# A two-layer decoder trunk: the split input at four offsets, and five small tiles allocated elsewhere

## Chip, cores and metric

The kernel runs on one core of a Trainium2 chip. The metric is the device time of one execution in microseconds (us). Of the kernel before, three runs are shown: 1055.95, 1058.14 and 1058.58 us, median 1058.14 us. One further execution was profiled; it took 1055.96 us.

## What is computed

Two layers (DEPTH = 2) over a sequence of 256 tokens of width 1024, all in float32. Each layer is a token mixer and a SwiGLU block, both with a residual and a LayerNorm:

```python
for l in range(DEPTH):
    h = _mixer(x, w_in[l], w_gla_a2[l], b_gla_a[l], gla_norm_g[l], ret_norm_g[l],
               w_branch[l], b_gate[l], w_out[l])
    x = _layer_norm(ALPHA * x + h, ln1_g[l], ln1_b[l])
    f = _swiglu(x, w_gate[l], w_up[l], w_down[l])
    x = _layer_norm(ALPHA * x + f, ln2_g[l], ln2_b[l])
```

The mixer multiplies x by one wide matrix `w_in` and feeds three branches from it (gated linear attention, retention, dilated window attention) and three gates of width 1024; the gated sum of the branches goes through `w_out`. So x is read as a matmul operand in four places, which this text calls stages: stage 0 is the mixer of layer 0, stage 1 the SwiGLU of layer 0, stage 2 the mixer of layer 1, stage 3 the SwiGLU of layer 1.

## The kernel before

**Split operands.** Every float32 matmul operand is held as two parts in the type F32R: a high part and what is left of it. A product takes three matmuls: high by high, high by low and low by high. The input x lies transposed (128 partitions, 8 blocks k of 256 tokens) in the two tiles XH and XL (lines 284 and 285), 8192 bytes of each partition. They are allocated once, and all four stages use them: at the start `start_split` fills them, and at the end of each sub-layer `ln_rest` (lines 439 to 470) writes the next stage's x over the old one. Matmuls reach them through `xh(k)` and `xl(k)` (lines 377 to 381).

**Weights.** They come in 340 units of 128 x 1024 by DMA through six staging tiles, and ScalarE and VectorE split each into a pair of blocks out of a ring of 24 (`r0` to `r23`, 4096 bytes of each partition each). The blocks lie directly behind each other, so all begin at the same place modulo 512 bytes.

**Two forms of matmul on x.** `a_pair` (line 408) holds a 128 x 128 piece of the weights in TensorE and moves x past it, 256 columns at a time; it serves the queries and keys of the dilated branch, the gates and most of the SwiGLU. `b_unit` (line 388) holds 128 tokens of x and moves the weights past it, 512 columns at a time:

```python
mm(o, hi[:, c0:c0 + 128], rh(k), start=(i == 0 and j == 0), stop=False)   # a_pair
mm(o, hi[:, c0:c0 + 128], rl(k), start=False, stop=False)
mm(o, lo[:, c0:c0 + 128], rh(k), start=False, stop=(i == n - 1 and j == 3))
...
mm(ps, a, wh, start=(k == 0), stop=False)                                 # b_unit
mm(ps, a, wl, start=False, stop=False)
mm(ps, b, wh, start=False, stop=(k == 2 * n - 1))
```

The second argument of `mm` is held, the third moves past it. Products without x have the same two forms: `a_pair` on the branch outputs (line 1014) and `down` (line 1094) move and hold blocks of the ring only. Every matmul is recorded on line 130 of the profile, every transpose on line 134, and work of VectorE and ScalarE on line 118, since helpers issue them.

**Order of work.** The program is written by hand in one order per engine; a small model of the engines' clocks (`issue`, `settle`, `tick`) decides while the program is built where the side work of the branches is put between the big products.

**The small tiles.** `half` and `one` hold constants (lines 365 and 367); `m0`, `m1`, `den0` and `den1` hold softmax maxima and sums, 48 bytes each (lines 894 and 895); `junk` (line 751 in the mixer's `gla_all`) takes the squares that nobody reads, when ScalarE sums them for a norm.

Of the kernel before, what the change touches and what calls it, by code (L numbers as in the profile page):

```python
# [9 lines left out]
F32R = mybir.dt.float32r  # L10
# [6 lines left out]
S = 256  # L17
L = 2
H = 4
FF = 2816  # L20
KT = D // 128
# [33 lines left out]
def trunk(ctx: ExitStack, tc: tile.TileContext, wst, xt_in, x_in, cst, tri, pcol, wga, wa2, lnp, out):  # L55
# [5 lines left out]
    def T(shape, tag, bufs=1, dt=F32):  # L61
        return sb.tile(shape, dt, tag=tag, name=tag, bufs=bufs)
# [65 lines left out]
    def mm(out, lhsT, rhs, **k):  # L128
        issue("P", [out], [lhsT, rhs], size(out) * (4 if lhsT.dtype == F32 else 1) / 2.4 + 3)
        return nc.tensor.matmul(out, lhsT, rhs, **k)  # L130

    def transpose(out, in_):
        issue("P", [out], [in_], size(out) * 2 / 2.4 + 3)
        return nc.tensor.transpose(out, in_, ident)  # L134
# [5 lines left out]
    def settle(*aps, margin=MARGIN):  # L140

        while any(when(written, a, "P") + margin > clk["P"] for a in aps):
            yield
# [95 lines left out]
    def free(u):  # L239
        assert u == state["freed"]  # L240
        R.put(*parts.pop(u))
        state["freed"] += 1
# [4 lines left out]
    def spawn(g):  # L247
        side.append(g)
# [32 lines left out]
            yield  # L281


    XH = T([128, KT, S], "xh", 1, F32R)
    XL = T([128, KT, S], "xl", 1, F32R)
    xts = [F2.main()[0] for _ in range(4)]


# [2 lines left out]
    def start_piece(i):  # L291
        a, b = PIECES[i]
        return a, b, xts[a // 2].rearrange("p (k t) -> p k t", k=2)[:, a % 2:a % 2 + b - a, :]
# [4 lines left out]

    def start_split(i):
        a, b, xs = start_piece(i)  # L300
        act(XH[:, a:b, :], xs, AF.Copy)
        stt(XL[:, a:b, :], xs, 1.0, XH[:, a:b, :].bitcast(F32), op0=OP.mult, op1=OP.subtract)

# [56 lines left out]
    def cs(name):  # L360
        a, b = COLS[name]
        return C[:, a:b]

    ident = cs("ident")
    half = T([128, 4], "half")
    V.memset(half, -0.5)
    one = T([128, 1], "one")
    V.memset(one, 1.0)
    gaT = T([49, S], "gaT")[32:49]
    V.memset(gaT, 1.0)  # L370
    def ln_params(l, which):
        g, b = F4.main(2)
        nc.scalar.dma_start(g[:, 0:D], lnp[l, 2 * which:2 * which + 1, :].partition_broadcast(128))
        nc.scalar.dma_start(b[:, 0:D], lnp[l, 2 * which + 1:2 * which + 2, :].partition_broadcast(128))
        return g, b

    def xh(k):
        return XH[:, k, :]

    def xl(k):  # L380
        return XL[:, k, :]


    def tokens(v, tt, dl):
# [13 lines left out]
    def b_group(units, lh, ll, tt, ps, dl=1, last=False):  # L398

        n = len(units)  # L400
        for i, u in enumerate(units):
            b_unit(u, i, n, lh, ll, tt, ps, dl)
            if last:
                free(u)
            if i < n - 1:
                tick()
# [27 lines left out]
    def ln_first(tt, c, ps, st):  # L434
        o = xres[:, tt, c * 512:c * 512 + 512]
        stt(o, o, ALPHA, ps, op0=OP.mult, op1=OP.add)
        V.bn_stats(st[:, c, :], o)

    def ln_rest(tt, st, gb, final):
        mv = T([128, 2], "mv", 2)  # L440
        V.bn_aggr(mv, st.rearrange("p a b -> p (a b)"))
        ve = T([128, 1], "ve", 2)
        ts(ve, mv[:, 1:2], 1e-5, None, op0=OP.add)
        rs = T([128, 1], "rs", 2)
        G.tensor_tensor(rs, ve, half[:, :1], op=OP.pow)
        g, b = gb
        for c in range(2):
            o = xres[:, tt, c * 512:c * 512 + 512]
            stt(o, o, mv[:, 0:1], g[:, c * 512:c * 512 + 512], op0=OP.subtract, op1=OP.mult)
        for c in range(2):  # L450
            o = xres[:, tt, c * 512:c * 512 + 512]
            stt(o, o, rs, b[:, c * 512:c * 512 + 512], op0=OP.mult, op1=OP.add)
            if final:
                nc.sync.dma_start(out[tt * 128:tt * 128 + 128, c * 512:c * 512 + 512], o)
        if tt == 1:
            F4.put(g, b)
        if final:
            return
        for c in range(2):
            yield from settle(xres[:, tt, c * 512:c * 512 + 512], margin=SHORT)  # L460
            (pt,) = yield from PS.get()
            for j in range(4):
                transpose(pt[:, j * 128:j * 128 + 128],
                                    xres[:, tt, c * 512 + j * 128:c * 512 + j * 128 + 128])
            src = pt.rearrange("p (j t) -> p j t", j=4)
            hi = XH[:, 4 * c:4 * c + 4, tt * 128:tt * 128 + 128]
            act(hi, src, AF.Copy)
            stt(XL[:, 4 * c:4 * c + 4, tt * 128:tt * 128 + 128], src, 1.0, hi.bitcast(F32),
                op0=OP.mult, op1=OP.subtract)
            PS.put(pt)  # L470
# [142 lines left out]
    def gla_gates(l, E):  # L613
        (pg,) = yield from PS.get()
        for k in range(KT):
            o = pg[0:16, 0:S]
            gh, gl = GH[:, l, k * 16:k * 16 + 16], GL[:, l, k * 16:k * 16 + 16]
            mm(o, gh, xh(k), start=(k == 0), stop=False)
            mm(o, gh, xl(k), start=False, stop=False)
            mm(o, gl, xh(k), start=False, stop=(k == KT - 1))  # L620
# [43 lines left out]
    def gla_all(l, E, pss, vb, sg):  # L664
# [4 lines left out]
        attz = []  # L669
# [36 lines left out]
        for n in range(3):  # L706
            tt, r0 = n // 2, (n % 2) * 64
# [21 lines left out]
        for tt in range(2):  # L729
            po = yield from PS.get(2)  # L730
            oh = [po[h % 2][:, (h // 2) * 128:(h // 2) * 128 + 128] for h in range(H)]
            for h in range(H):
                o = oh[h]
                a0 = ((h % 2) * 2 + h // 2) * 128
                mm(o, attz[tt][:, a0:a0 + 128], val[:, tt, h * 128:h * 128 + 128], start=True, stop=True,
                   skip_group_check=True)
                for c in range(2):
                    n = 2 * tt + c
                    if n == 0:
                        continue  # L740
                    r0 = (h % 2) * 64
                    mm(o[c * 64:c * 64 + 64, :], qk[r0:r0 + 64, h // 2, n * 64:n * 64 + 64],
                       Ss[n][r0:r0 + 64, h // 2, :], start=False, stop=True, skip_group_check=True)
            ss = T([128, H], "gss", 2)
            jk = T([128, 128], "junk")
            for h in range(H):
                act(jk, oh[h], AF.Square, accum_out=ss[:, h:h + 1])
            ts(ss, ss, 1.0 / 128, 1e-6, op0=OP.mult, op1=OP.add)
            rs = T([128, H], "grs", 2)
            G.tensor_tensor(rs, ss, half, op=OP.pow)  # L750
            for h in range(H):
                g = sg[:, tt * 512 + h * 128:tt * 512 + h * 128 + 128]
                stt(g, oh[h], rs[:, h:h + 1], g, op0=OP.mult, op1=OP.mult)
            PS.put(*po)
            F2.put(attz[tt])
            yield
# [136 lines left out]
    for l in range(L):  # L893
# [100 lines left out]
        for d in range(4):  # L994
            tg = []
            for br in range(3):
# [3 lines left out]
                t = F2.main()[0]  # L1000
# [34 lines left out]
        ln1 = ln_params(l, 0)  # L1035
        us = take(8)
        for tt in range(2):
            st = T([128, 2, 6], "lnst", 2)
            for c in range(2):
                ps = PM.main()[0]  # L1040
                state["calm"] = c == 1
                b_group(us[4 * c:4 * c + 4], lambda k: MM[k // 4][0][:, (k % 4) * 256:(k % 4) * 256 + 256],
                        lambda k: MM[k // 4][1][:, (k % 4) * 256:(k % 4) * 256 + 256], tt, ps, last=tt == 1)
                ln_first(tt, c, ps, st)
                PM.put(ps)
                if c == 1:
                    spawn(ln_rest(tt, st, ln1, False))
                tick()
                state["calm"] = False
        R.put(*MM[0], *MM[1])  # L1050


        state["cap"] = (NR - 5) // 2
# [36 lines left out]
        ln2 = ln_params(l, 1)  # L1090
# [24 lines left out]
        for p in range(NPAIR):  # L1115
# [3 lines left out]
            t = F2.main()[0]  # L1119
# [24 lines left out]
        final = l == L - 1  # L1144
        for tt in range(2):

            st = T([128, 2, 6], "lnst", 2)
            for cc in ((0,), (1,)) if tt else ((0, 1),):
                for i, u in enumerate(last_us):
                    state["calm"] = i > 2 and 1 in cc  # L1150
                    down(u, pend[i // 2], i % 2, tt, False, i == len(last_us) - 1, cc)
                    if cc == (1,):
                        free(u)
                    if 1 not in cc or i < len(last_us) - 1:
                        tick()
                for c in cc:
                    ln_first(tt, c, acc[tt, c], st)
            PS.put(acc[tt, 0], acc[tt, 1])
            spawn(ln_rest(tt, st, ln2, final))
            tick()  # L1160
            state["calm"] = False
        R.put(*pend)
    while side:
        tick()

# [153 lines left out]
```

## Time and profile before

| | |
|---|---|
| median of three runs | 1058.14 us |
| the profiled execution's own time | 1055.96 us |
| its span, first to last instruction | 1054.1 us |
| TensorE matmul busy | 1044.4 us (99%) |
| VectorE, ScalarE, GpSimd busy | 66%, 46%, 2% |
| mean granted TensorE clock | 0.998 |
| DMA, mean over the span | 182 GB/s |

The span is what the profile shows of the program; the 1.9 us around it belong to the execution. "Busy" of TensorE counts a matmul from its start to a modelled end, and neighbours overlap, so 99% busy does not say how fast the matmuls follow each other. That is read from the distance of their starts, called the pace here: the time from one matmul's start to the next one's.

### The profile page before, as it was taken

How to read it: one execution, taken by the hardware profiler on the slowest of the kernel's cores; microseconds unless marked ns; L12 is line 12 of the kernel's file. 1: busy time of each engine (PE TensorE's matmuls, PEld its weight loads, DVE VectorE, ACT ScalarE, POOL GpSimd, SP SyncE). 2: the span in 40 equal slices, each digit the busy share in tenths (PEclk: the TensorE clock that was granted, in tenths of full speed). 3: DMA queues.
4: the chain of work that ended last, by engine and by line, in shares of the span. 5: the costliest groups of instructions: out<-in, count | busy, mean ns of one | idle time of the engine just before them, and what ended most of it. 6: DMA issues, size and time to landing. Idle time of an engine off the chain costs nothing.

```text
span 1054.1 us, 17500 instructions
## 1 busy us (share of the span) xinstructions
PE 1044.4 (99%) x7122; PEld 953.9 (90%) x7122; DVE 695.3 (66%) x1066; ACT 485.5 (46%) x733; POOL 17.9 (2%) x24
## 2 busy tenths in 40 slices
PE   9999999999999999999999999999999999999997
PEld 7999987799998899999889999878999988999995
DVE  6688755767658755454688767477676686555454
ACT  6565554444344444344364554644434544444330
POOL 0000000000000000000000000000000000000000
PEclk9999999999999999999999999999999999999999
DMA  9676633437556575555376456343366657555521
GB/s 343 228 275 200 205 109 128 140 99 237 185 179 216 187 259 183 193 191 193 121 272 207 143 164 201 110 136 129 121 205 196 192 199 250 200 200 178 192 91 40
DMA packets 55666, 192.25 MB, mean 182 GB/s; under 512 B 6257, under 2 KB 7409, under 8 KB 55586
## 3 DMA queue, kind: packets, MB, share of 16 engines
q1 hardware_dynamic: 50400, 180.38, 51.5%
q10 hardware_dynamic: 5186, 10.76, 3.0%
q8 instruction: 56, 0.92, 0.4%
q14 instruction: 24, 0.20, 0.1%
HBM read 187.93 MB, written 3.18 MB: 181 GB/s over the span
## 4 chain that ended last, share of the span: by engine, by line
PE 99%; DMA 0%; DVE 0%; SPq 0%; issue 0%; DVEq 0%; ACT 0%
PE pm L130 77%; PE px L130 19%; PE px L134 2%; DMA stage<-in_wst_dram 0%; DVE xres L118 0%; SPq L138 0%; DVE lnst L118 0%; DVE r L118 0%; DVEq L1314 0%; ACT r L118 0%; DVE mv L118 0%; DVE ve L118 0%
## 5 line engine op out<-in xcount | busy, mean ns | idle before, releaser
L130 PE MATMUL pm<-xh,r 128*128 128x256 f32 x2688 | 478.9, 280 | 0.0
L118 DVE SCALAR_TENSOR_TENSOR r<-stage,r 128x1024 fp32r<-128x1024 f32 (+1 forms) x341 | 401.9, 1214 | 41.4 <-ACT r L118 39.4
L130 PEld LDWEIGHTS pm<-xh,r 128*128 128x128 f32 x2688 | 413.3, 189 | 1.1
L118 ACT ACTIVATE r<-stage 128x1024 fp32r<-128x1024 f32 (+1 forms) x327 | 332.6, 1051 | 96.8 <-PE pm L130 36.6
L130 PE MATMUL pm<-xl,r 128*128 128x256 f32 x1344 | 374.9, 279 | 0.0
L130 PEld LDWEIGHTS pm<-xl,r 128*128 128x128 f32 x1344 | 252.7, 188 | 0.8
L130 PE MATMUL pm<-r,xh 128*128 128x512 f32 x672 | 215.2, 401 | 0.8 <-ACT r L118 0.6
L130 PEld LDWEIGHTS pm<-r,xh 128*128 128x128 f32 x672 | 123.4, 190 | 29.4 <-issue 3.0
L130 PE MATMUL pm<-r,xl 128*128 128x512 f32 x336 | 132.2, 393 | 0.0
L130 PE MATMUL px<-r,r 128*128 128x512 f32 x528 | 122.6, 389 | 0.0
L130 PEld LDWEIGHTS px<-r,r 128*128 128x128 f32 x528 | 97.9, 188 | 19.3
L130 PE MATMUL pm<-r,r 128*128 128x256 f32 (+1 forms) x768 | 115.4, 310 | 0.0
L130 PEld LDWEIGHTS pm<-r,r 128*128 128x128 f32 x768 | 105.3, 190 | 7.3
L118 DVE SCALAR_TENSOR_TENSOR f<-f,pm 128x512 f32<-128x512 f32 x52 | 35.6, 685 | 110.9 <-ACT f L118 94.2
L118 ACT ACTIVATE f<-pm 128x512 f32<-128x512 f32 x72 | 42.6, 593 | 131.3 <-PE pm L130 129.4
L130 PEld LDWEIGHTS pm<-r,xl 128*128 128x128 f32 x336 | 63.7, 190 | 13.8
L118 ACT ACTIVATE r<-f 128x512 fp32r<-128x512 f32 x28 | 17.7, 632 | 96.6 <-DVE f L118 96.6
L130 PE MATMUL px<-f,f 128*128 128x128 f32 (+4 forms) x368 | 59.2, 301 | 0.0
L130 PEld LDWEIGHTS px<-f,f 128*128 128x128 f32 (+2 forms) x368 | 47.9, 183 | 9.7 <-issue 3.4
L118 ACT ACTIVATE f<-px 128x512 f32<-128x512 f32 (+2 forms) x52 | 25.2, 505 | 45.2 <-PE px L130 26.5
L118 ACT ACTIVATE f<-pm,hcol 128x256 f32<-128x256 f32 x48 | 20.1, 471 | 55.4 <-PE pm L130 55.3
L118 DVE TENSOR_TENSOR f<-f,pm 128x512 f32<-128x512 f32 x22 | 15.1, 687 | 41.0 <-PE pm L130 40.8
(102 smaller groups left out, 484.8 us busy)
## 6 DMA issues: line engine op xcount, KB each, us to landing
stage<-in_wst_dram SPq DMA_DIRECT2D x339, 512.0 KB, 4.5
f<-in_lnp_dram ACTq DMA_DIRECT2D x8, 512.0 KB, 7.0
scr<-f ACTq DMA_DIRECT2D x8, 260.0 KB, 3.4
f<-scr ACTq DMA_DIRECT2D x4, 520.0 KB, 3.7
xres<-in_x_dram ACTq DMA_DIRECT2D x4, 256.0 KB, 5.3
out_dram<-xres SPq DMA_DIRECT2D x4, 256.0 KB, 2.0
f<-in_xt_dram SPq DMA_DIRECT2D x3, 256.0 KB, 7.9
cst<-in_cst_dram ACTq DMA_DIRECT2D x4, 192.0 KB, 4.0
```

The source lines that it names most:

```text
L118: return f(*a, **k)
L130: return nc.tensor.matmul(out, lhsT, rhs, **k)
L134: return nc.tensor.transpose(out, in_, ident)
```

## The change

XH and XL become larger tiles (8 x 256 plus 80 elements), and each stage uses a window of them that begins at its own offset `PHASE`: 0, 64, 80 and 32 elements, which is 0, 256, 320 and 128 bytes. `stage[0]` counts the stages while the program is built; `xh` and `xl` read the current stage's window, and `ln_rest` writes the next one's. The tiles `den0` and `den1` are allocated ahead of the first, `half`, `one`, `m0` and `m1` between the two, so that both begin at the same place modulo 512 bytes. `junk` is dropped: the squares go into the first 128 columns of `attz[tt]`, a block that the matmuls before them have read.

```diff
-    XH = T([128, KT, S], "xh", 1, F32R)
-    XL = T([128, KT, S], "xl", 1, F32R)
+    PHASE = (0, 64, 80, 32)
+    for n in ("den0", "den1"):
+        T([128, 3, H], n)
+    XB = [T([128, KT * S + max(PHASE)], "xh", 1, F32R)]
+    half = T([128, 4], "half")
+    one = T([128, 1], "one")
+    for n in ("m0", "m1"):
+        T([128, 3, H], n)
+    XB.append(T([128, KT * S + max(PHASE)], "xl", 1, F32R))
+    XS = [[x[:, p:p + KT * S].rearrange("p (k t) -> p k t", k=KT) for x in XB] for p in PHASE]
+    stage = [0]
...
     def xh(k):
-        return XH[:, k, :]
+        return XS[stage[0]][0][:, k, :]
     def xl(k):
-        return XL[:, k, :]
+        return XS[stage[0]][1][:, k, :]
...
-    def ln_rest(tt, st, gb, final):
+    def ln_rest(tt, st, gb, final, nxt=None):
...
+        XH, XL = XS[nxt]
...
-            jk = T([128, 128], "junk")
+            jk = attz[tt][:, 0:128]
...
-                    spawn(ln_rest(tt, st, ln1, False))
+                    spawn(ln_rest(tt, st, ln1, False, 2 * l + 1))
...
+        stage[0] += 1
...
-            spawn(ln_rest(tt, st, ln2, final))
+            spawn(ln_rest(tt, st, ln2, final, 2 * l + 2))
...
+        stage[0] += 1
```

In the built programs the places are these, in bytes of each partition. The blocks `r0` to `r23` begin at 128 modulo 512 in both. XH began at 164416 and XL at 172608, both 64 modulo 512. Now the tiles begin at 164544 and 173248, both 192 modulo 512, and the windows of stages 0 to 3 begin at 192, 448, 0 and 320 modulo 512. This text calls the start of x less the start of a block, modulo 512 bytes, the **distance**:

| | stage 0 | stage 1 | stage 2 | stage 3 |
|---|---|---|---|---|
| before | 448 | 448 | 448 | 448 |
| now | 64 | 320 | 384 | 192 |

A product of two blocks of the ring, without x, has distance 0 in both.

No instruction moves on any engine, and no instruction of TensorE waits for another engine than before. What differs in the rows is the place of the squares on ScalarE, here at the end of gated linear attention in layer 0 (`px` are PSUM tiles, `gss` the sums, `f_100` and `f_105` the two blocks of `attz`):

```order
-L118 ACTIVATE junk,gss<-px_109 128x128
-L118 ACTIVATE junk,gss<-px_110 128x128
...
+L118 ACTIVATE f_100,gss<-px_109 128x128
+L118 ACTIVATE f_100,gss<-px_110 128x128
...
 L118 ACTIVATE f_94<-pm_108 128x512
...
+L118 ACTIVATE f_105,gss<-px_111 128x128
+L118 ACTIVATE f_105,gss<-px_112 128x128
```

The squares stand at the same place in ScalarE's order and only write elsewhere.

## Rows read from the trace of the kernel before

**Rows 1.** The page: TensorE's busy time, granted clock by slice, the last chain.

```profile
PE 1044.4 (99%) x7122; PEld 953.9 (90%) x7122; DVE 695.3 (66%) x1066; ACT 485.5 (46%) x733; POOL 17.9 (2%) x24
...
PEclk9999999999999999999999999999999999999999
...
PE 99%; DMA 0%; DVE 0%; SPq 0%; issue 0%; DVEq 0%; ACT 0%
```

**Rows 2.** Waits of TensorE: who waited for whom, us in total, times, longest.

```profile
PE px L130 <- DVE f L118: 1.4, 1, 1.4
```

**Rows 3.** The page's groups: operation, out<-in, shapes, count | busy us, mean ns | idle.

```profile
L130 PE MATMUL pm<-xh,r 128*128 128x256 f32 x2688 | 478.9, 280 | 0.0
L130 PE MATMUL pm<-xl,r 128*128 128x256 f32 x1344 | 374.9, 279 | 0.0
L130 PE MATMUL pm<-r,xh 128*128 128x512 f32 x672 | 215.2, 401 | 0.8 <-ACT r L118 0.6
L130 PE MATMUL pm<-r,xl 128*128 128x512 f32 x336 | 132.2, 393 | 0.0
```

**Rows 4.** Timeline of TensorE, stage 0's gates: start us, length us, engine, operation, count.

```profile
257.06 0.28 PE L130 MATMUL pm<-xl,r 128*128 128x256 f32 x1
...
259.78 0.28 PE L130 MATMUL pm<-xl,r 128*128 128x256 f32 x1
```

**Rows 5.** Timeline of TensorE, stage 1, the last pairs of the SwiGLU.

```profile
495.91 0.28 PE L130 MATMUL pm<-xl,r 128*128 128x256 f32 x1
...
507.57 0.28 PE L130 MATMUL pm<-xl,r 128*128 128x256 f32 x1
```

**Rows 6.** Timeline of TensorE, stage 0: a product of two ring blocks.

```profile
260.00 8.78 PE L130 MATMUL pm<-r,r 128*128 128x256 f32 x72
```

**Rows 7.** Groups by shape within 270 to 283 us (stage 0, the gates).

```profile
L130 PE MATMUL pm<-xh,r 128*128 128x256 f32 x78 | 13.3, 276 | 0.0
```

**Rows 8.** Groups by shape within 28 to 58 us (stage 0, first queries and keys).

```profile
L130 PE MATMUL pm<-xh,r 128*128 128x256 f32 x128 | 22.8, 281 | 0.0
```

**Rows 9.** Groups by shape within 383 to 510 us (stage 1).

```profile
L130 PE MATMUL pm<-xh,r 128*128 128x256 f32 x512 | 91.6, 281 | 0.0
L130 PE MATMUL pm<-xl,r 128*128 128x256 f32 x256 | 71.9, 281 | 0.0
```

**Rows 10.** Groups by shape within 846 to 1054.1 us (stage 3).

```profile
L130 PE MATMUL pm<-xh,r 128*128 128x256 f32 x576 | 102.9, 281 | 0.0
```

**Rows 11.** Groups by shape within 1 to 325 us (stage 0).

```profile
L130 PE MATMUL pm<-xh,r 128*128 128x256 f32 x768 | 136.9, 280 | 0.0
L130 PE MATMUL pm<-xl,r 128*128 128x256 f32 x384 | 106.8, 278 | 0.0
```

**Rows 12.** Groups by shape within 523 to 846 us (stage 2).

```profile
L130 PE MATMUL pm<-xh,r 128*128 128x256 f32 x768 | 136.1, 279 | 0.0
L130 PE MATMUL pm<-xl,r 128*128 128x256 f32 x384 | 106.5, 277 | 0.0
```

**Rows 13.** Timeline of TensorE, stage 2: eight transposes, then x.

```profile
588.61 1.03 PE L134 MATMUL px<-cst,f 128*128 128x128 f32 x8
589.40 0.36 PE L130 MATMUL pm<-xh,r 128*128 128x256 f32 x1
589.61 0.28 PE L130 MATMUL pm<-xl,r 128*128 128x256 f32 x1
```

**Rows 14.** Timeline of TensorE, 512 columns: two ring blocks; then weights past x, twice.

```profile
509.93 13.76 PE L130 MATMUL px<-r,r 128*128 128x512 f32 x60
...
343.77 0.39 PE L130 MATMUL pm<-r,xl 128*128 128x512 f32 x1
...
346.52 0.39 PE L130 MATMUL pm<-r,xl 128*128 128x512 f32 x1
...
93.01 0.39 PE L130 MATMUL pm<-r,xl 128*128 128x512 f32 x1
...
97.21 0.40 PE L130 MATMUL pm<-r,xl 128*128 128x512 f32 x1
```

More of the change, by code (lines that the diff above doesn't have):

```diff
@@ L300, in start_split @@
         a, b, xs = start_piece(i)
+        XH, XL = XS[0]
         act(XH[:, a:b, :], xs, AF.Copy)
@@ L364, in trunk @@
     ident = cs("ident")
-    half = T([128, 4], "half")
     V.memset(half, -0.5)
-    one = T([128, 1], "one")
     V.memset(one, 1.0)
```

## The prediction

> **What bounds the kernel.** I read the page first. The chain that ended last is TensorE for 99% of the span, TensorE is busy 1044.4 of 1054.1 us, and the granted clock stands at its upper level, 2.4 GHz, in every slice [rows 1]. The waits come next: the longest wait of TensorE for another engine is 1.4 us, once [rows 2]. So no engine, transfer or clock is left to take the blame. The time is the number of matmuls by the pace at which they follow each other, and the change leaves the number and the order alone. What I must read is the pace, from the starts in the timeline, and whether it hangs on addresses.
>
> It is not one pace. With 256 columns of x, 24 matmuls start between 257.06 and 259.78 us, 113.3 ns each [rows 4]. In the SwiGLU the same form takes 11.66 us for 33 groups of three, so 99 matmuls at 117.8 ns [rows 5]. And 72 matmuls of 256 columns on ring blocks alone need 8.78 us; less the last one's 0.28, that is 71 steps of 119.7 ns [rows 6]. The shape is the same in all three and no wait lies in any. I call these paces fast, middle and slow. The groups by shape let one tell them apart over long stretches, since the modelled length of a matmul moves with its pace: 276 ns where it is fast [rows 7], 281 where it is middle [rows 8, 9].
>
> Two things separate them. One is where the operands lie: products at distance 0 run slow, those on x, at distance 448, never do for long. The other is what ran just before: stage 0 reads x at one address throughout, yet has 281 ns between 28 and 58 us [rows 8] and 276 between 270 and 283 [rows 7]. A pace, once taken, lasts for dozens of matmuls. My reading is that the read of the moving operand and the load of the next held one get in each other's way, by a fixed amount, according to their relative place and the moment at which each starts. That is an inference from the three paces, and no row shows the collision itself.
>
> **The change part by part.** *Offsets, 256 columns.* 4032 matmuls of this form read x, with mean lengths 280 and 279 ns [rows 3]. What they lose against the fast pace:
> - Stage 1 has 768 at 281 ns [rows 9], so 768 x (117.8 - 113.3) = 3.4 us. Stage 3 runs the same program at the same lengths [rows 10]: 3.4 us again. Together 6.8 us.
> - The mixers, by length above 276: stage 0 has 768 x 4 + 384 x 2 = 3.8 us [rows 11], stage 2 has 768 x 3 + 384 x 1 = 2.7 us [rows 12]. A part of these 6.5 us is not pace: the first matmul after eight transposes is 0.36 us long and holds the next one back to 0.21 us after it [rows 13], and such a start remains wherever x lies.
>
> So at most 13.3 us are lost here. The other end is all 4032 at the slow pace: 4032 x (119.7 - 113.3) = 25.8 us lost, 12.5 more than now.
>
> *Offsets, 512 columns.* Here the weights move past a held piece of x: 672 + 336 matmuls [rows 3]. Ring blocks alone step by (13.76 - 0.39) / 59 = 226.6 ns; with x held, 12 take 2.75 us, 229.2 ns, in one place and 18 take 4.20 us, 233.3 ns, in another [rows 14]. The loss now is between 1008 x 2.6 = 2.6 us and 1008 x 6.7 = 6.8 us, so a move is worth from -6.8 to (all at 233.3, from 2.6 now) +4.2 us.
>
> *Which values I take.* No row shows distances 64, 192, 320 or 384, so the ends are those above: -20.1 us (13.3 + 6.8) and +16.7 us (12.5 + 4.2). I decide by the nearest rows. Distance 0 is slow all along; 448, which is 64 bytes off, is already fast in about half of the mixers' stretches. Three of the four new distances (192, 320, 384) lie further from 0 than 448 does, and I expect them to collide less. Only stage 0's 64 is as near, on the other side. For the SwiGLU stages, at 320 and 192, I take nine tenths of the loss: 6.1 us. For the mixers I take a third of 6.5 us, 2.2 us, as the starts after transposes stay and stage 0 is uncertain. For 512 columns, half of the lower loss: 1.3 us. Sum: 9.6 us.
>
> *Small tiles and squares.* Moving five tiles of at most 48 bytes adds no instruction. The squares now write into a block whose readers on TensorE have finished when the sums they square are ready; TensorE waits for ScalarE nowhere that the longest wait of 1.4 us doesn't bound [rows 2]. I price it at nothing, covered by TensorE's own queue of matmuls; if that cover failed in all four places (two token tiles, two layers), four such waits would cost 5.6 us.
>
> *Sum.* The profiled execution took 1055.96 us, 1.9 us more than its span, and 1055.96 - 9.6 = 1046.4. It is the fastest but for 0.01 us of the executions shown, and the median of the three runs is 2.2 us higher; against that median I forecast 1058.14 - 9.6 = 1048.5 us.
>
> **Rivals.** *Place does not matter.* The paces would then come from what runs before alone, and as the order stays, so does the time: 1058 us. For it speaks that one address shows two paces [rows 7, 8]. Against it: products at distance 0 have a pace of their own, 119.7 ns, that neither stretch on x shows [rows 4 to 6], while nothing else in their form differs. The Trainium skill takes this rival's side twice. Its page "SBUF — State Buffer", section "SBUF: two separate sides", says that TensorE has its own ports and never waits there, and "TensorE: Matmul & The Clock Gate", section "Step-by-step: what each phase is for", gives it two independent read ports, for the moving and the held operand. By these the change would be worth nothing. The second page's "Back-to-back issue gap" would allow N/2.4 + 2.5 ns, which is 109.2 for 256 columns; no row reaches that, the trace has 113.3 to 119.7, so I don't rely on it.
>
> *The new distances collide more.* A stage whose distance makes every load meet the moving read takes the slow pace from end to end, as distance 0 does. It decides once more than about half of the 4032 matmuls run slow (13.3 of 25.8 us). Stage 2 alone at the slow pace adds 1152 x 6.4 - 2.7 = 4.7 us, which gives 1063 us with the rest unchanged; all four stages give 1058.1 + 12.5 = 1071 us. For it speaks that the entry into each stretch matters and is unknown; against it, that only distance 0 shows the slow pace for long.
>
> *Part of the gain.* One SwiGLU stage turns fast, the other stays at the middle pace, and the mixers give a little: 3.4 + 1.0 = 4.4 us, so 1053.7 us.
>
> **How the numbers follow.** About 0.3%, 3.2 us here, is what a measurement of this kernel can tell from no change. The forecast, a gain of 6 to 14 us, has a chance of 0.52, the partial gain 0.20: faster 0.72. Place without effect: 0.17. Slower by the collision: 0.11. The lower end of the range is nearly all that can be had without the starts after transposes: 6.8 us in the SwiGLU, two thirds of the mixers' (4.3) and the lower loss of the 512 columns (2.6), 13.7 us, so 1044.4 us. The upper end goes past the partial gain to a time without change, 1059 us. Outside lie the slower cases, half of what is left of "no change" above 1059, and a few hundredths below.
>
> **What would show it.** In the changed profile the SwiGLU's groups on x should read 276 ns instead of 281, and their starts 113.3 ns apart; the mixers' means should fall towards 276 with 0.36 us still on the first after transposes; 512 columns with x held should step nearer to 226.6. Ring blocks alone must stay at 119.7 and 226.6. The prediction is wrong if the SwiGLU keeps 281 (place doesn't matter) or shows 283 (more collisions), and its sum is wrong if the pace falls below 113.3, which I hold to be the floor.

## The result, and the profile after

The changed kernel takes 1066.55 us in the median of four runs, beside 1057.05 us for the kernel before on the same chip: 1.0090 times the time, 95% interval 1.0078 to 1.0102. It is slower by 9.5 us, where a gain of 9.6 us was forecast. Its profiled execution took 1065.53 us.

The profile of the changed kernel first: the span, the engines' busy time and the groups of matmuls on x, as in [rows 1, 3].

```profile
span 1063.7 us, 17497 instructions
...
PE 1053.9 (99%) x7122; PEld 962.1 (90%) x7122; DVE 695.6 (65%) x1066; ACT 485.7 (46%) x733; POOL 17.9 (2%) x24
...
L130 PE MATMUL pm<-xh,r 128*128 128x256 f32 x2688 | 486.7, 281 | 0.0
...
L130 PE MATMUL pm<-xl,r 128*128 128x256 f32 x1344 | 376.4, 280 | 0.0
...
L130 PE MATMUL pm<-r,xh 128*128 128x512 f32 x672 | 215.8, 402 | 0.6 <-ACT r L118 0.3
...
L130 PE MATMUL pm<-r,xl 128*128 128x512 f32 x336 | 132.4, 394 | 0.0
```

The counts are those of before, VectorE and ScalarE are as busy as they were, and TensorE is busy 9.5 us longer. Next its waits (who waited for whom, us in total, times, longest), as in [rows 2]:

```profile
PE px L130 <- DVE f L118: 1.4, 1, 1.4
...
PE px L130 <- DVE r L118: 0.4, 1, 0.4
```

One wait of 0.4 us is new to the list, so the loss is no wait either. It is pace: summed over the starts in both traces, the matmuls of 256 columns on x take 7.8 of the 9.6 us more (2.7, 0.4, 4.7 and 0.0 in stages 0 to 3), and those of 512 columns 1.5 (0.7, 0.4, 0.4 and 0.0). The stages tell where. Each stage is taken here from the first matmul on x to that of the next stage. These are the starts of stages 1, 2 and 3 in the timeline of TensorE (start us, length us, engine, operation, count), in the kernel before:

```profile
341.25 0.62 PE L130 MATMUL pm<-r,xh 128*128 128x512 f32 x2
...
527.16 0.62 PE L130 MATMUL pm<-r,xh 128*128 128x512 f32 x2
...
861.56 0.62 PE L130 MATMUL pm<-r,xh 128*128 128x512 f32 x2
```

and in the changed kernel, the same three:

```profile
344.68 0.63 PE L130 MATMUL pm<-r,xh 128*128 128x512 f32 x2
...
531.66 0.64 PE L130 MATMUL pm<-r,xh 128*128 128x512 f32 x2
...
871.14 0.62 PE L130 MATMUL pm<-r,xh 128*128 128x512 f32 x2
```

From these and the ends of the spans (1054.1 and 1063.7 us):

| us | stage 0 | stage 1 | stage 2 | stage 3 | sum |
|---|---|---|---|---|---|
| before | 341.25 | 185.91 | 334.40 | 192.54 | 1054.1 |
| changed | 344.68 | 186.98 | 339.48 | 192.56 | 1063.7 |
| difference | +3.43 | +1.07 | +5.08 | +0.02 | +9.6 |

The mixers (stages 0 and 2) lose most, one SwiGLU loses a little, and stage 3 is unchanged (0.02 us, where the spans are known to 0.1) although its distance went from 448 to 192. That last entry is the clue to the rest.

Pace in the changed kernel, from the starts in TensorE's timeline. First the gates of stage 0, 33 matmuls from one row to the other, then the gates of stage 2, 24 matmuls:

```profile
258.02 0.28 PE L130 MATMUL pm<-xl,r 128*128 128x256 f32 x1
...
261.91 0.28 PE L130 MATMUL pm<-xl,r 128*128 128x256 f32 x1
...
798.56 0.28 PE L130 MATMUL pm<-xl,r 128*128 128x256 f32 x1
...
801.41 0.28 PE L130 MATMUL pm<-xl,r 128*128 128x256 f32 x1
```

3.89 us / 33 = 117.9 ns where [rows 4] had 113.3, and 2.85 us / 24 = 118.7 ns, a pace that the kernel before does not show. The groups of stage 2 (527 to 855 us), as in [rows 12], agree in direction:

```profile
L130 PE MATMUL pm<-xh,r 128*128 128x256 f32 x768 | 140.8, 283 | 0.0
L130 PE MATMUL pm<-xl,r 128*128 128x256 f32 x384 | 108.0, 281 | 0.0
```

Both means rose by 4 ns, from 279 and 277. The groups of stage 3 (855 us to the end) are those of [rows 10], busy time included:

```profile
L130 PE MATMUL pm<-xh,r 128*128 128x256 f32 x576 | 102.9, 281 | 0.0
```

With 512 columns and x held, at the place where [rows 14] had 229.2 ns (the start of stage 1), 21 matmuls now take 4.90 us, 233.3 ns; ring blocks alone, in the last row, take (13.80 - 0.39) / 59 = 227.3 ns, where 226.6 stood. The prediction wanted these unchanged; the excess lies in the first seven after x, which follow each other in 225 to 240 ns, and from there on it is 227 as before:

```profile
345.15 0.40 PE L130 MATMUL pm<-r,xl 128*128 128x512 f32 x1
...
350.05 0.40 PE L130 MATMUL pm<-r,xl 128*128 128x512 f32 x1
...
514.41 13.80 PE L130 MATMUL px<-r,r 128*128 128x512 f32 x60
```

### The profile page after: what moved, and what is told of

It is laid out like the page before. It is cut to its first block, busy times and chain, and to the rows that moved or that the text cites. A ratio compares the mean times of both kernels' runs of the same rounds, so it can differ in the third digit from the quotient of the medians.

```text
span 1063.7 us, 17497 instructions
## 1 busy us (share of the span) xinstructions
PE 1053.9 (99%) x7122; PEld 962.1 (90%) x7122; DVE 695.6 (65%) x1066; ACT 485.7 (46%) x733; POOL 17.9 (2%) x24
## 4 chain that ended last, share of the span: by engine, by line
PE 98%; DMA 0%; DVE 0%; SPq 0%; ACT 0%; issue 0%; DVEq 0%
PE pm L130 77%; PE px L130 19%; PE px L134 2%; DMA stage<-in_wst_dram 0%; DVE xres L118 0%; SPq L138 0%; DVE r L118 0%; ACT r L118 0%; DVE lnst L118 0%; DVEq L1326 0%; DVE mv L118 0%; DVE ve L118 0%
## 5 line engine op out<-in xcount | busy, mean ns | idle before, releaser
L130 PE MATMUL pm<-xh,r 128*128 128x256 f32 x2688 | 486.7, 281 | 0.0
L118 ACT ACTIVATE f<-px 128x512 f32<-128x512 f32 (+3 forms) x68 | 29.6, 452 | 56.9 <-PE px L130 36.2
```

Source lines behind the costliest of these rows:

```text
L118: return f(*a, **k)
```

## Experiments

The first question was whether the loss lies in the offsets alone or in the small tiles and squares too, and which place has which pace. The second was why the SwiGLU ran at the middle pace in the kernel before.

### One place for all four stages

Four kernels keep the larger tiles, the windows and the squares in `attz` of the change and give all stages the same place. Of the small tiles only `m0` stays between XH and XL; `half` and `one` follow XL, and `den0`, `den1` and `m1` are allocated where the kernel before does it. In this layout XH and XL both begin at 64 modulo 256 bytes, with the ring at 128. Below, "step" of a kernel or a stage is the start of x less the start of a ring block modulo **256** bytes.

```diff
-    PHASE = (0, 64, 80, 32)
-    for n in ("den0", "den1"):
-        T([128, 3, H], n)
-    XB = [T([128, KT * S + max(PHASE)], "xh", 1, F32R)]
+    PHASE = (0, 0, 0, 0)        # d192; (16,) * 4 is d0, (32,) * 4 is d64, (48,) * 4 is d128
...
+    XB = [T([128, KT * S + 48], "xh", 1, F32R)]
+    T([128, 3, H], "m0")
+    XB.append(T([128, KT * S + 48], "xl", 1, F32R))
     half = T([128, 4], "half")
     one = T([128, 1], "one")
-    for n in ("m0", "m1"):
-        T([128, 3, H], n)
-    XB.append(T([128, KT * S + max(PHASE)], "xl", 1, F32R))
```

> All stages at distance 192 modulo 256 (x at one place, as before); small tiles moved and the squares put into attz, as in the change. If the pace hangs on the distance modulo 256 alone, this is the time of before: ratio 0.997 to 1.003, and every stage as long as before. If the small tiles or the squares made the loss, it stays at the changed kernel's 1.009.

> As d192, with x at distance 0 modulo 256 in all stages. If the distance decides: 256-column matmuls on x take the pace of ring blocks, 119.7 ns (mean length 283), 6 ns more than the fast pace on 4000 of them, and the 512-column ones take 226.6; together 11 us slower than before, ratio 1.010. If only what runs before decides: ratio 1.000.

> As d192, with x at distance 64 modulo 256 in all stages, which stages 0 and 1 of the changed kernel have. If the distance modulo 256 decides: stages 0 and 1 as long as in the changed kernel (3.4 and 1.1 us more than before), stage 2 about as stage 0, stage 3 as stage 1: 9 us slower, ratio 1.009. If what runs before decides: ratio 1.000.

> As d192, with x at distance 128 modulo 256 in all stages, which stage 2 of the changed kernel has. If the distance modulo 256 decides: stage 2 as in the changed kernel (5.1 us more than before), stage 0 nearly the same, the SwiGLU stages 1 to 2 us more each: 12 us slower, ratio 1.011. If what runs before decides: ratio 1.000.

| kernel | step | ratio to before (95%) | stage 0 | stage 1 | stage 2 | stage 3 |
|---|---|---|---|---|---|---|
| d192 | 192 | 0.9998 (0.9989 to 1.0008) | 340.68 | 185.91 | 334.17 | 192.54 |
| d64 | 64 | 1.0099 (1.0084 to 1.0114) | 344.92 | 186.98 | 338.76 | 193.64 |
| d0 | 0 | 1.0146 (1.0129 to 1.0163) | 348.79 | 188.18 | 339.90 | 194.83 |
| d128 | 128 | 1.0155 (1.0140 to 1.0170) | 346.14 | 188.66 | 339.66 | 195.34 |

Stage lengths in us are taken from the timelines as above. In d192 the starts of stages 1 to 3 are these:

```profile
340.68 0.62 PE L130 MATMUL pm<-r,xh 128*128 128x512 f32 x2
...
526.59 0.62 PE L130 MATMUL pm<-r,xh 128*128 128x512 f32 x2
...
860.76 0.62 PE L130 MATMUL pm<-r,xh 128*128 128x512 f32 x2
```

Stage 0 also holds the start of the program, which is not equally long in all executions: the first matmul of 256 columns on x starts at 29.17 us in the kernel before and at 31.64 us in d0. And the 192 matmuls that follow ran at the middle pace in the kernel before [rows 8] and at the fast one in d192, at the same step. So stage 0 is compared from the first matmul of 512 columns behind these 192, here in the kernel before, d192, the changed kernel and d64:

```profile
51.78 0.63 PE L130 MATMUL pm<-r,xh 128*128 128x512 f32 x2
...
51.21 0.63 PE L130 MATMUL pm<-r,xh 128*128 128x512 f32 x2
...
52.02 0.63 PE L130 MATMUL pm<-r,xh 128*128 128x512 f32 x2
...
52.26 0.63 PE L130 MATMUL pm<-r,xh 128*128 128x512 f32 x2
```

From there to stage 1 it is 289.47 us in the kernel before and in d192, 292.66 us in the changed kernel and in d64, 293.71 in d128 and 294.12 in d0. Taken so, d0 loses 4.7 us in stage 0, not the 7.5 of the table.

d192 has the squares and the larger tiles of the changed kernel and the time of the kernel before, so these parts cost nothing, and the loss lies in the offsets. The small tiles lie elsewhere in d64 than in the changed kernel, with the same 292.66 us, so their place costs nothing there either. With the distances of the change read modulo 256, the stages have the steps 64, 64 (320), 128 (384) and 192. Put against the table, each stage of the changed kernel has the length that its own step gives: stage 0 344.68 beside 344.92 in d64, stage 1 186.98 beside 186.98, stage 2 339.48 beside 339.66 in d128, stage 3 192.56 beside 192.54 in d192. And the kernel before, at 448, had step 192 throughout. The totals of d0 and d128 lie above what was expected (1.010 and 1.011), with 2.3 to 2.8 us lost in each SwiGLU.

The paces, from two starts each in the timelines of TensorE. d64, the gates of stage 0, 33 matmuls in 3.89 us, 117.9 ns:

```profile
257.88 0.28 PE L130 MATMUL pm<-xl,r 128*128 128x256 f32 x1
...
261.77 0.28 PE L130 MATMUL pm<-xl,r 128*128 128x256 f32 x1
```

d0, stage 1, 42 matmuls in 5.03 us, 119.8 ns:

```profile
496.79 0.28 PE L130 MATMUL pm<-xl,r 128*128 128x256 f32 x1
...
501.82 0.28 PE L130 MATMUL pm<-xl,r 128*128 128x256 f32 x1
```

d128, stage 1, 39 matmuls in 4.68 us, 120.0 ns; its gates in stage 0, in the last two rows, take 4.28 us for 36, 118.9 ns:

```profile
494.97 0.28 PE L130 MATMUL pm<-xl,r 128*128 128x256 f32 x1
...
499.65 0.28 PE L130 MATMUL pm<-xl,r 128*128 128x256 f32 x1
...
258.82 0.28 PE L130 MATMUL pm<-xl,r 128*128 128x256 f32 x1
...
263.10 0.28 PE L130 MATMUL pm<-xl,r 128*128 128x256 f32 x1
```

So over the long stretches the fast pace stands at step 192 alone. One short stretch goes the other way. In the changed kernel, at step 64, 45 matmuls of stage 0 take 5.10 us, 113.3 ns, and so they do in d64, while the same stretch runs at the middle pace in the kernel before and in d192:

```profile
65.83 0.28 PE L130 MATMUL pm<-xl,r 128*128 128x256 f32 x1
...
70.93 0.28 PE L130 MATMUL pm<-xl,r 128*128 128x256 f32 x1
```

Step 64 has a fast pace too, then, but nearly no stretch of this program takes it. With 512 columns the order of the places is another: at the start of stage 1 in d0, 21 matmuls with x held take 4.75 us, 226.2 ns, as little as ring blocks alone, where the kernel before had 229.2 and the changed kernel 233.3:

```profile
349.25 0.39 PE L130 MATMUL pm<-r,xl 128*128 128x512 f32 x1
...
354.00 0.39 PE L130 MATMUL pm<-r,xl 128*128 128x512 f32 x1
```

The modelled lengths, which told fast from middle in the kernel before, do not tell the new paces apart: in the changed kernel the gates have a mean of 279 ns in stage 0, at 117.9, and of 281 in stage 2, at 118.7, the length that stood for 117.8 in [rows 5, 9]. Only the starts do.

### Is it the place of x, or its place against the ring?

d192's offsets, with 64 bytes allocated ahead of the ring, so that ring and x both move by 64 bytes:

```diff
+    T([128, 16], "pad")
     R = Blocks(...)
...
+    PHASE = (0, 0, 0, 0)
+    XB = [T([128, KT * S + 64], n, 1, F32R) for n in ("xh", "xl")]
```

> As d192, with a tile of 64 bytes ahead of the ring: ring blocks and x both lie 64 bytes further, so the distance stays 192 while x lies at the address modulo 256 that it has in d0. If the distance between x and the blocks decides: ratio 0.998 to 1.002 to before, mean length of 256-column matmuls on x as in d192. If the place of x by itself decides: the time of d0, ratio 1.014.

Measured: 0.9999 (0.9990 to 1.0009). x now begins where it has step 0 against the old ring, and the groups of stage 2 (523 to 846 us) are within 0.4 us of [rows 12]:

```profile
L130 PE MATMUL pm<-xh,r 128*128 128x256 f32 x768 | 136.5, 279 | 0.0
L130 PE MATMUL pm<-xl,r 128*128 128x256 f32 x384 | 106.6, 278 | 0.0
```

The place relative to the ring decides; the address of x by itself does not.

### Steps between, and XH and XL apart

Two questions that could lead to a better place: whether a step of 32 bytes off the four finds one, and whether XH and XL count separately. On the layout of the run before, without its `pad`:

```diff
+    PHASE = (8, 8, 56, 56)      # fine32: steps 224, 224, 160, 160
...
+    PHASE, PHASEL = (0, 0, 0, 0), (16, 16, 32, 32)     # xl_apart_a: XH 192; XL 0, 0, 64, 64
+    PHASE, PHASEL = (0, 0, 32, 32), (48, 48, 0, 0)     # xl_apart_b: XH 192, 192, 64, 64; XL 128, 128, 192, 192
```

> Distances off the steps of 64 bytes: 224 in stages 0 and 1, 160 in stages 2 and 3. If what counts is in which 64 bytes a column lies, each stage lies between its neighbours: stage 0 between 52.7 (192) and 60.8 (0) and stage 2 between 47.7 (192) and 53.2 (128) us over the floor; the total then is 1057 to 1072 us. If a read that begins off a step of 64 costs a line more on every matmul (7 ns on 4000), 1080 us and more.

> XH at distance 192 in all stages, XL at 0 in stages 0 and 1 and at 64 in stages 2 and 3. If each matmul pays by its own distance: in the SwiGLU two of three lose 4.0 ns and one 6.6 (stage 1) or 4.5 (stage 3), 4.9 and 4.2 ns in the mean; total 1058 to 1062 us. If the pace of a whole stretch is set by its three matmuls together, a stage can fall to the fast pace or leave it altogether: the SwiGLU's means move by more than 2 ns from these.

> Stages 0 and 1: XH at distance 192, XL at 128. Stages 2 and 3: XH at 64, XL at 192. If each matmul pays by its own distance: SwiGLU means of (4.0 + 4.0 + 6.5) / 3 = 4.8 ns in stage 1 and (4.5 + 4.5 + 4.0) / 3 = 4.3 ns in stage 3, mixers 2.6 and 3.4 ns; total 1060 to 1066 us. If the three together set the pace: off by more than 2 ns.

| kernel | ratio to before (95%) | stage 0 | stage 1 | stage 2 | stage 3 |
|---|---|---|---|---|---|
| fine32 | 1.0136 (1.0115 to 1.0156) | 347.58 | 187.48 | 339.40 | 194.34 |
| xl_apart_a | 1.0092 (1.0072 to 1.0112) | 346.16 | 186.36 | 338.61 | 193.27 |
| xl_apart_b | 1.0108 (1.0088 to 1.0128) | 346.92 | 187.38 | 338.34 | 192.96 |

Neither 160 nor 224 is better than 192; each stage lies between those of the neighbouring steps in the table above, as expected. With XL alone elsewhere stage 2 loses 4.4 us: 338.61 us beside 334.17 in d192 and 338.76 with both at step 64, although only one matmul in three moves XL. Both totals lie above the sums one by one (1066.18 us beside 1058 to 1062, 1067.91 beside 1060 to 1066). So in the mixers the parts do not add up one by one: one operand at a bad place takes the triple, and with it the stretch, out of the fast pace. In the SwiGLU, which at step 192 is at the middle pace already, the means over the starts stay within 1 ns of these sums counted from 113.3 (118.0 and 117.9 ns in stages 1 and 3 of xl_apart_a, 118.8 and 117.2 in xl_apart_b), so there the sign that was set for a common pace did not come.

### What the entry into a stretch does

Step 192 has the fast pace in the mixers and the middle one in the SwiGLU [rows 4, 5], so place is not the whole. The SwiGLU's stretches of 96 matmuls (the last of a layer has 192) each follow a product of ring blocks. This kernel puts one more matmul ahead of 14 of them, seven in each layer, each with another number of columns, from 8 to 240. It writes into columns that the next matmul overwrites.

```diff
+KICK = ({1: 8, 2: 16, 3: 32, 4: 48, 5: 64, 6: 96, 7: 128},
+        {1: 144, 2: 160, 3: 176, 4: 192, 5: 208, 6: 224, 7: 240})
...
-    def a_pair(units, rh, rl, ps):
+    def a_pair(units, rh, rl, ps, kick=0):
...
                 hi, lo = touch(u)
+                if kick and a == 0 and i == 0:
+                    nc.tensor.matmul(ps[:, 0:kick], hi[:, 0:128], rh(0)[:, 0:kick], start=True, stop=True)
...
-            a_pair(ug, xh, xl, pg)
+            a_pair(ug, xh, xl, pg, KICK[l].get(p, 0))
```

> d192 with one added matmul at the head of 14 stretches of the SwiGLU (the pairs 1 to 7 of each layer, each of which follows a down product on ring blocks): 8, 16, 32, 48, 64, 96 and 128 columns in layer 0, 144 to 240 in steps of 16 in layer 1, of the first weights by the first block of x, into the bank that the next matmul overwrites; the output does not change. In d192 these stretches all run at the middle pace (281 ns). If the moment of entry sets the pace and a stretch keeps it, some of the 14 turn to the fast pace over their 96 matmuls (mean 276 ns, 0.42 us less each) and the others stay; total 1052 to 1058 us. If the middle pace belongs to the SwiGLU's operands, all 14 stay at 281 and the time is 1 us longer by the added matmuls.

Measured: 1.0000 (0.9989 to 1.0012). The timeline of two neighbouring stretches in stage 1, each from the added matmul (line 421) to the next product of ring blocks:

```profile
438.57 0.18 PE L421 MATMUL pm<-xh,r 128*128 128x48 f32 x1
...
449.98 5.62 PE L131 MATMUL px<-r,r 128*128 128x512 f32 x24
...
455.45 0.19 PE L421 MATMUL pm<-xh,r 128*128 128x64 f32 x1
...
466.46 0.86 PE L131 MATMUL px<-r,r 128*128 128x512 f32 x3
```

After 48 columns the stretch takes 11.41 us, after 64 columns 11.01 us. Of the 14 stretches three turned fast, after 64, 96 and 192 columns; the others kept the middle pace. The three gain 3 x 96 x 4.5 ns = 1.3 us, and the fourteen added matmuls cost more than that: stages 1 and 3 are together 0.5 us longer than in d192. So the total does not show it.

### The entry put to use, at the old place and at the new ones

The same edit with 64 columns ahead of all fourteen stretches, once on d192's offsets and once on the changed kernel itself:

```diff
+KICK = ({p: 64 for p in range(1, 8)}, {p: 64 for p in range(1, 8)})
```

> d192 with the added matmul of 64 columns at the head of all 14 stretches, which turned its stretch fast in kick_scan. If entry sets the pace: all 14 run fast, 12 x 0.40 us and 2 x 0.83 us less, 6.5 us in all, ratio 0.993 to 0.995 to before. If the turn in kick_scan was luck of that place: some stay at 281 and the ratio lies between 0.995 and 1.000.

> The changed kernel with the same added matmuls. Its stage 1 has distance 320 (64 modulo 256), its stage 3 distance 192. If a fast pace exists at 192 alone: stage 3's stretches turn to 276 ns and stage 1's stay at 281, 3.2 us less than the changed kernel, ratio 1.006 to before. If entry alone decides, whatever the distance: both turn, 6.5 us less, ratio 1.003.

kick64 takes 1051.61 us beside 1056.40: 0.9950 (0.9937 to 0.9964), less than either kernel. All 14 stretches are fast. Its groups of stage 1 (325 to 520 us), where [rows 9] had 281 ns:

```profile
L131 PE MATMUL pm<-xh,r 128*128 128x256 f32 x576 | 100.3, 278 | 0.0
...
L131 PE MATMUL pm<-xl,r 128*128 128x256 f32 x288 | 79.6, 276 | 0.0
```

Stage 1 takes 183.52 us and stage 3 190.24, which is 2.39 and 2.30 us less than before, together 4.7 us. The 4.8 us of the median agree. Expected were 6.5 us, which left out what the added matmuls themselves take.

kick64_changed takes 1065.92 us, 1.0091 (1.0077 to 1.0105). One stretch of stage 1 (step 64) and one of stage 3 (step 192), in its timeline:

```profile
427.68 0.19 PE L425 MATMUL pm<-xh,r 128*128 128x64 f32 x1
...
439.10 1.08 PE L131 MATMUL px<-r,r 128*128 128x512 f32 x4
...
953.22 0.19 PE L425 MATMUL pm<-xh,r 128*128 128x64 f32 x1
...
964.24 1.08 PE L131 MATMUL px<-r,r 128*128 128x512 f32 x4
```

11.42 us and 11.02 us: the added matmul helps at step 192 and not at step 64. Stage 1 became 0.7 us longer (187.68 us), stage 3 2.4 us shorter (190.19). The total does not show this gain of 1.7 us, and neither of the ratios expected (1.006 and 1.003) came. In the profiled execution it was lost in stage 0, where nothing was edited and which took 347.51 us instead of 344.68, all of it ahead of the first matmul of 256 columns on x (at 32.25 us instead of 29.41). The rows below show its start: nine matmuls of 512 columns from the first row to the second take 427 ns each, and nine from the third to the fourth 233 ns.

```profile
8.81 0.63 PE L131 MATMUL pm<-r,xl 128*128 128x512 f32 x1
...
12.65 0.63 PE L131 MATMUL px<-r,xl 128*128 128x512 f32 x1
...
13.82 0.39 PE L131 MATMUL px<-r,xl 128*128 128x512 f32 x1
...
15.92 0.39 PE L131 MATMUL pm<-r,xl 128*128 128x512 f32 x1
```

The changed kernel had its full pace from 7.5 us on. The profile gives a granted clock of 1.00 for these microseconds in both kernels, so it does not tell why. Whether the same happened in the timed runs no profile shows. Their ratio and that of the changed kernel are known to 0.0014 and 0.0012, 1.5 and 1.3 us, so a gain of 1.7 us can hardly be told; why the median misses it stays open.

## Why the prediction was wrong

**The bound was right.** Only TensorE's pace matters: the loss of 9.5 us is 9.5 us of TensorE busy time with the same matmuls.

**Small tiles and squares were right.** Priced at nothing. d192 has the squares and measures 0.9998. The small tiles (six by the diff, where five are spoken of) lie elsewhere in d64 than in the changed kernel, and from the same matmul on stage 0 takes 292.66 us in both.

**That place matters was right**, and the rival that it doesn't is out: from the best to the worst step tried the whole time goes from 0.9998 to 1.0155. The Trainium skill's "SBUF — State Buffer", section "SBUF: two separate sides", has TensorE never waiting there, and "TensorE: Matmul & The Clock Gate", section "Step-by-step: what each phase is for", gives it independent ports for the moving and the held operand. For this kernel the runs differ: the same program, with x moved by 64 bytes against the weights, takes 1.5% more.

**The step that failed is "Which values I take".** It ordered the distances by how far they lie from 0, modulo 512, and expected 192, 320 and 384 to collide less than 448. Three things were wrong in it.
- The period is 256 bytes, not 512. Stage 3's 192 is the old place again, and its term of the gain (half of 6.1 us) measured 0.02 us. Stage 1's 320 is the same place as stage 0's 64.
- Pace does not grow better with distance from 0. Of the steps tried, 192 alone has the fast pace in the long stretches; 64 and 128, as far from 0 or further, have 117.9 and 118.9 to 120.0 ns there, and d128, the furthest, is as slow as d0. I had taken the old place for a half bad one, since only half of its stretches were fast. It was the best of those tried, so each of the new places could only lose or draw.
- The SwiGLU's middle pace, 6.8 us that the sum meant to win by place, came from the entry into its stretches. I had written that what ran just before separates the paces too, but then priced the whole of that loss as place. kick64 shows the other reading: same place, another entry, 4.7 us less. Of a stretch of 96, 11.01 - 96 x 0.1133 = 0.13 us goes to the added matmul and the entry, 1.9 us over fourteen, which is most of what is left of the 6.8.

**The mixers' term** had the wrong sign: -2.2 us forecast for the matmuls of 256 columns on x, +7.4 measured for them (2.7 + 4.7; the two stages as wholes lose 3.43 + 5.08 = 8.5).

**The 512 columns' term**, -1.3 us, had the wrong sign too: at the start of stage 1 the pace went from 229.2 to 233.3 ns, and 96 x 4.1 = 0.4 us is what the 96 of the stage lose, of its 1.07 us. Summed over the starts it is +1.5 us, 0.7 of them in stage 0 together with the start of the program. For this form the prediction's own rows spoke against its order of distances: ring blocks alone, at distance 0, gave the floor of the term, 226.6 ns [rows 14], and with x at step 0 the runs show 226.2 there.

**The rival that came true** is "the new distances collide more", with 0.11. Its price for stage 2 alone was 4.7 us, and 4.7 of the 5.08 measured there lie in the matmuls that it priced. That agreement is in part luck: it expected the slow pace (119.7), and what came was 118.7 in the gates there, with 117.9 in stage 0, whose fast stretches went too. Its argument against itself, that only distance 0 shows the slow pace for long, held for the one distance that the trace offered besides the old one. Two points of a curve were seen, and the shape of the curve was guessed.

**The collision itself** remains an inference. The runs show that the pace hangs on the relative place modulo 256 bytes, in the mixers on all operands of the triple, and on how a stretch is entered. Which two accesses meet, no row shows.

## What to carry to other kernels

When TensorE is never idle and equal matmuls run at several paces, move one operand against the other in steps of 64 bytes and time each whole kernel; four kernels settled it here, where a guess from one place did not. Before leaving a place that is fast in part, look whether it is fast anywhere else: if it is, the slow stretches may owe their pace to their entry, and a short matmul ahead of them is the cheaper thing to try. Read paces from the distance of starts, not from modelled lengths, and undo the parts of a change that are "free" in a run of their own, so that the rest can be blamed with certainty.

## What the runs showed of the hardware that was not expected

- Matmuls of 256 columns in F32R ran at 113.3, 117.9, 118.7 to 118.9 and 119.8 to 120.0 ns according to where the moving operand lay against the held one, modulo 256 bytes, and to how the stretch was entered (113.3 and about 117.8 both stand at step 192 and at step 64); moving both operands by 64 bytes changed nothing (0.9999).
- With one added matmul of 64 columns ahead of 96 others the stretch took 11.01 us, itself included, beside 11.41 after one of 48 columns, and the fast pace lasted for the whole stretch. Of 14 column counts from 8 to 240, only 64, 96 and 192 did so, and at step 64 an added matmul of 64 columns did not.
- With 512 columns and x held, step 0 had the best pace at the start of stage 1 (226.2 ns, beside 229.2 at step 192 and 233.3 at 64).
- Moving XL alone, which is moved by one matmul in three, cost stage 2 of the mixers about as much as moving both (338.61 and 338.76 us, from 334.17).
